# Matmuls of an S5 mixer regrouped by their shape on TensorE

## The chip, the core and the metric

The kernel runs on one core of a Trainium2 chip. The metric is the device time of one execution in microseconds (us); the median of three runs before the change is 2721.66 us (2709.77 to 2725.01). The engines are named as in the profile: PE is TensorE's matmul, PEld its weight load, DVE VectorE, ACT ScalarE, POOL GpSimd, SP the queue that issues most DMAs.

## The reference

One layer of a hybrid decoder for 1024 prompt tokens and 8 single-token samples, of width 1024:

```python
h = x + 0.5 * gt1 * swiglu(modulate(rmsnorm(x)))
proj = modulate(rmsnorm(h)) @ w_in              # S5 inputs, RWKV inputs, gates
y_s5 = s5_branch(proj[..., :512])               # 32 groups of 16 channels, 64 complex states each
y_rwkv = rwkv_branch(token_shift(proj[..., 512:2304]))
m = sigmoid(gates_a) * y_s5 + sigmoid(gates_b) * y_rwkv
h = h + gt2 * (m @ w_out)
h = h + 0.5 * gt3 * swiglu(modulate(rmsnorm(h)))
y = rmsnorm(h)
```

The S5 branch, which the change touches, is a diagonal complex recurrence per group g, with state n and channel c:

```python
bu = einsum('blgc,gnc->blgn', ug, bb)           # complex
xs[t] = lam_bar * xs[t - 1] + bu[t]             # scan over the tokens
y = real(einsum('blgn,gcn->blgc', xs, C)) + d * u
out = (gelu(y) @ glu_v) * sigmoid(gelu(y) @ glu_g)
```

## The kernel before, in words

The kernel works through FFN 1, the input projection, the S5 mixer, the RWKV-7 mixer, the merge and FFN 2. All large products go through `dense` (L144): each product is three matmuls of 128x128 weights against 344 columns (L152 to L154). They are called dense matmuls below. The program's instructions are put on each engine's queue by a scheduler: it takes the code's order with priorities and fills an engine with work of lower priority while something of higher priority isn't ready. Each queue then runs in order.

The S5 mixer (`s5_mix`, L706) works on chunks of 8 tokens: 128 chunk rows of the prompt, and a few rows more for the samples. It runs four quarters of 8 groups each (`s5_quarter`, L616). The tiles of a quarter are single-buffered, and its PSUM tiles come from one tag of four slots. A quarter goes through these steps:

- X transposes and Xs transposes (L628 to L633, recorded at L160): for each of the 8 groups one 128x128 transpose of the prompt (X) and one of 16 rows (Xs), alternating, into three PSUM tiles, each evacuated by ACT (L634).
- State inputs (L640): 16 matmuls with 64 weight columns, evacuated by ACT (L642).
- On DVE the rotation, the scan and the rotation back (L647 to L664), which give the states H. The real half of H is ready after L661, the imaginary one after L664.
- Output products. For each parity g2 of the group (two loops of 4 groups), in PSUM tiles `py` for the prompt and `pz` for the samples: one product of the chunk's own inputs (L687, all 128 rows of the array), two of H (L689, real and imaginary part, 64 rows; the parity says which half of the partitions), then the same three for the samples with 8 weight columns (L691, L693). So the shape on the array changes with nearly every instruction.
- DVE adds the product to `X` (L697) and to the sample rows (L702); ACT applies gelu.

After the quarters, `s5_mix` transposes the result Z (recorded at L160, too) and writes it out. A product in fp32 appears as two records of PE each (x2), a transpose as one. While the S5 mixer runs, PE's queue is filled up with dense matmuls of the RWKV projections (`rwkv_tiles`, called at L1500), which stand behind S5 in the code; their evacuations on ACT and DVE, the tiles `gate`, are raised above S5's work (`offset=30000`), and so stand between the S5 instructions on DVE. When S5 is over, its pool is closed and the RWKV mixer starts (L1510).

Of the kernel before, what the change touches and what calls it, by code (L numbers as in the profile page):

```python
# [19 lines left out]
PSUM = bass.MemoryType.PSUM  # L20
# [5 lines left out]
NP = 1024            # prompt tokens  # L26
NB = 8               # sample sequences
T = NP + NB          # columns
CH = T // 3          # column chunk (one PSUM bank)
LP = NP - 2 * CH     # prompt columns in the last chunk  # L30
# [11 lines left out]
def host_consts():  # L42
    """Identity, ones and masks; they depend on shapes alone."""
    r = np.arange(P)[:, None]
    c = np.arange(P)[None, :]
    c64 = np.arange(64)[None, :]
    m = r % 64
    up = lambda k: (((c64 >> k) - (m >> k)) == 1) & ((c64 >> (k + 1)) == (m >> (k + 1)))
    d = {
        "ident": r == c,  # L50
        "ones": np.ones((P, P)),
        "bones": r // 64 == c // 64,
        "su": r % 64 < c64,
        "ui": r % 64 <= c64,
        "up": np.concatenate([up(4), up(5)], axis=1),
        "i64": m == c64,
    }
    cf = np.concatenate([d[n].astype(np.float32) for n, _ in CF], axis=1)
    return np.ascontiguousarray(cf)
# [6 lines left out]
class Net:  # L66
# [51 lines left out]
    def split(self, hi, lo, src):  # L118
        """hi + lo = src exactly, both with 12 significant bits."""
        nc = self.nc  # L120
        nc.scalar.copy(hi, src)  # L121
        nc.vector.tensor_sub(lo, src, hi.bitcast(F32))  # L122

    def wload(self, *srcs, pool=None):
        """One weight unit of at most 1024 columns as (hi, lo); srcs stack along the middle."""
# [14 lines left out]
    def wcols(self, w, j, n=P):  # L140
        """Column block j of w[(k p), f] as [p, k, n]."""
        return self.wload(w[:, j * n:(j + 1) * n].rearrange("(k p) f -> p k f", p=P))

    def dense(self, terms, c, cols=None):  # L144
        """terms: list of (wh, wl, xh, xl) with [K,128] and [K,cols]; returns PSUM."""
# [11 lines left out]
    def tr(self, out, in_):  # L157
        """out[M, K] = in_[K, M] transposed through the tensor engine."""
# [31 lines left out]
    def ada_steps(self, strips, pool):  # L190
        """Modulation columns of up to four 512-wide strips, side by side in the array; one step per k."""
# [24 lines left out]
    def norm_params(self, q, ks):  # L216
        """a = g (1 + scale) of norm q for the feature tiles ks."""
# [16 lines left out]
    def rsqrt(self, pt, scale, eps_col, pool, floor=None, n=CH, m=P, tmp=None):  # L234
        """1/sqrt(scale * pt + eps) (or of max(pt, floor)), refined by one Newton step."""
# [30 lines left out]
    def norm_apply(self, h, q, c, rs, xh, xl, pool):  # L266
        """One chunk of xh + xl = modulate(rmsnorm(h)) for norm q."""
# [23 lines left out]
    def norm_steps(self, h, q, pool, params=True):  # L291
        """scale(c, tag) and apply(c, xh, xl) of norm q, to be called chunk by chunk."""
# [9 lines left out]
    def resid(self, h, hin, pt, g, d, c):  # L302
        """h[d] = hin[d] + pt * g over one chunk."""
# [12 lines left out]
    def ffn(self, h, q, w1, w3, w2, xh, xl, gp, groups, hooks=None, wp2=None, wide=None):  # L316
        """h += gate * (silu(x w1) * (x w3)) w2 for the hidden tiles of some groups.

        wide: the order of a group's steps: "Hc.e" the hidden products of a chunk, "Oc" its output.
        """  # L320
# [39 lines left out]
    def load_x(self, h, g, pool):  # L360
        """Token tiles 3 g .. 3 g + 2 (the last group ends with the samples), transposed into h."""
# [24 lines left out]
    def final_out(self, h, c, pool, gf):  # L386
        """rmsnorm(h) * g_final for one chunk of tokens, turned token-major first."""
# [28 lines left out]
    def exp_small(self, out, x, pool, n):  # L416
        """exp(x) by range reduction and a polynomial (fp32 accuracy)."""
# [42 lines left out]
    def cmul(self, ore, oim, are, aim, bre, bim, t1, eng=None):  # L460
        """(ore, oim) = a * b; outputs must not alias inputs."""
# [9 lines left out]
    def s5_prep(self, sp):  # L471
        """Discretised parameters; the wide ones go to DRAM scratch by quarters of 8 groups."""
# [9 lines left out]
        # [(g2 n), gp] views of lam_re, lam_im and log_dt  # L482
# [30 lines left out]
        # k = (lam_bar - 1) / lam  # L513
# [15 lines left out]
        # powers lam_bar^tau, tau = 0..8, and the same reversed (7 - s)  # L529
# [12 lines left out]
        # bb[(g2 n), gp, c]  # L542
# [7 lines left out]
        # C as [(g2 n), gp, c]  # L550
# [14 lines left out]
        for g in range(16):  # L565
            nc.sync.dma_start(self.sK[:, 2 * g:2 * g + 2, 0:112], zer)
            # lam^(7-s) bb -> transposed
# [12 lines left out]
            # C lam^tau, sign folded into the imaginary part  # L580
# [6 lines left out]
            # K_tau[c, c']  # L587
# [10 lines left out]
            # e^{i 8 ang q}, q = 0..127  # L598
# [13 lines left out]
    def s5_quarter(self, qd, X, Xs, us, Z, h0, zs, dbc, pool, tag):  # L612
# [15 lines left out]
        for g0, gn in ((0, 3), (3, 3), (6, 2)):  # L628
            pt = self.t(self.pp, [P, gn, 144], tag)
            for q in range(gn):  # L630
                g = 8 * qd + g0 + q
                self.tr(pt[:, q, 0:128], X[:, g].rearrange("p s c -> p (s c)"))
# [33 lines left out]
        # sample states: lam_bar h0 + bb u  # L666
# [8 lines left out]
        # outputs; one PSUM bank per parity of the group, as the parities use different row tiles  # L675
# [4 lines left out]
        xsq = Xs[0:NB, :, 0, :].rearrange("p (gp g2) c -> p g2 gp c", g2=2)  # L680
        for g2 in range(2):
            py = self.t(self.pp, [P, 4, P], tag)
            pz = self.t(self.pp, [NB, 4, 16], tag)
            rows = slice(64 * g2, 64 * g2 + 64)
            for gp in range(4):
                g = 2 * gp + g2
                nc.tensor.matmul(py[:, gp, :], uT[:, g, 0:P], mi[:, g, :], start=True, stop=False)  # L687
                for z in range(2):
                    nc.tensor.matmul(py[:, gp, :], H[rows, gp, z, 0:P],  # L689
                                     co[rows, gp, z, 1:9, :].rearrange("p t c -> p (t c)"), start=False, stop=z == 1)  # L690
                nc.tensor.matmul(pz[:, gp, :], uT[:, g, 128:136], mi[:, g, 0:16], start=True, stop=False)  # L691
                for z in range(2):
                    nc.tensor.matmul(pz[:, gp, :], h0q[rows, z, gp, :], co[rows, gp, z, 1, :],  # L693
                                     start=False, stop=z == 1)
            xv = Xq[:, g2]
            nc.gpsimd.tensor_mul(xv, xv, dq[:, g2].unsqueeze(2).to_broadcast([P, 4, 8, 16]))
            v.tensor_add(xv, xv, py.rearrange("p g (t c) -> p g t c", t=8))  # L697
            for gp in range(4):
                cc = c0 + 32 * gp + 16 * g2
                nc.scalar.activation(Z[:, :, cc:cc + 16], X[:, 8 * qd + 2 * gp + g2], AF.Gelu_apprx_tanh)  # L700
            v.tensor_mul(zq[:, g2], xsq[:, g2], dq[0:NB, g2])
            v.tensor_add(zq[:, g2], zq[:, g2], pz)  # L702
# [3 lines left out]
    def s5_mix(self, X, usT, zout, pool, tag="mm"):  # L706
        """X [128 q, 32 g, 8 s, 16 c] chunk-major inputs, usT [128, 4, 8]; zout(ct, tile) gets z transposed."""
# [12 lines left out]
        # sample rows, once as the first and once as the last token of a chunk  # L720
# [29 lines left out]
        # states out  # L750
# [11 lines left out]
    def rw_init(self, rows, keep, tag):  # L762
        """Per-feature vectors and low-rank weights."""
# [19 lines left out]
    def rw_clear(self, pool):  # L783
        """Zeros around the diagonal blocks of the inverses' scratches."""
# [8 lines left out]
    def rw_lora(self, wad, gd):  # L793
        """wad rows: 64 of wd, 64 of ad; gd: 128 rows (mixed, [128, T])."""
# [6 lines left out]
    def inv_half(x, h):  # L801
        """[64, 4, 64] view of head h; the heads of a scratch lie 4160 apart."""
# [3 lines left out]
    def inv_diag(x):  # L806
        """[32, 16, 16] view of the diagonal blocks of a scratch."""
        return x.rearrange("(q r) -> q r", r=1040)[:, 0:1024].rearrange("q (t s) -> q t s", s=64)[:, :, 0:16]

    def rw_decay(self, sw, tmp, r, exps):  # L810
        """exps(fm, fp, r): r (1 - t)^2 and r (1 + t)^2 are exp(-y), exp(y) for y = e^-0.5 sw and t = tanh(y/2)."""
# [3 lines left out]
        # 1 / (1 - t^2) = (1 + t^2)(1 + t^4)(1 + t^8)(1 + t^16), t < 0.295  # L815
# [13 lines left out]
    def rw_part(n):  # L829
        """Tokens of step n, and its two head pairs with their columns in the step's tiles."""  # L830
# [3 lines left out]
    def rw_prep(self, n, pool):  # L834
        """Decay products, normalised keys and the like for two chunks each of two head pairs."""
# [43 lines left out]
    def rw_solve(self, n, q, pool):  # L879
        """Products of the rows a, r with the rows b, k of four chunks, and the inverses of I - A's 16-blocks.  # L880

        The state is carried without the decay of its last chunk, which a and r take up.  Head h's feature rows
        sit on its own half of the partitions with b's token rows; k's and v's token rows sit on the other.
        """
# [38 lines left out]
        # the 16 x 16 diagonal blocks, one per partition  # L923
# [28 lines left out]
    def rw_quad(self, n, q, sv, pool):  # L952
        """b, k and v with their tokens in the rows, the bonus, and the whole inverse."""
# [6 lines left out]
        # v of each head in the columns of the other half, next to columns that nothing reads  # L960
# [18 lines left out]
        # bonus  # L979
# [8 lines left out]
        # (I - A)^-1 = X P1 P2 from the inverse X of the diagonal blocks, with P1 = I + A1 X and P2 = I + A2 X P1 for  # L988
        # the blocks A1 next to them and A2 below; Y is the transpose
# [604 lines left out]
```

## Time and profile before

| | |
|---|---|
| runs | 2709.77, 2721.66, 2725.01 us |
| span of the profiled execution | 2725.0 us |
| PE busy | 2635.2 us, 97% |
| DVE busy | 1521.9 us, 56% |
| ACT, POOL busy | 804.8 us, 464.3 us |
| mean granted clock of PE over the span | 0.970 of full |
| S5 quarters on PE, first transposes to last product | 1016.90 to 1166.09 us |

The span is as long as the slowest of the three runs (2725.01 us), so nothing of note lies around it. In a timeline each line gives the start and the length of an instruction or of a merged group, engine, line, operation, tiles, weight shape (rows*columns), moving shape and the number of records. Lengths of matmuls overlap, since they are pipelined; what one costs in a full queue is the distance from its start to the start of the next line.

### The profile page before, as it was taken

The page shows a single profiled execution, that of the slowest core. Times are in us where ns is not written, and L with a number is a line of the kernel's source. Part 1 is how long each engine was busy: PE and PEld are TensorE (multiplying, and loading weights), DVE is VectorE, ACT ScalarE, POOL GpSimd, SP SyncE. Part 2 cuts the span into 40 slices and gives each one's busy share as a digit, 9 for nine tenths or more (in the row PEclk, how much of TensorE's full clock was granted, in tenths as well). Part 3 has the DMA queues.
Part 4 walks back from the last instruction along what each step waited for, and adds up shares of the span by engine and source line. Part 5 has one row for each costly group of instructions (what it writes and reads, how often), then busy time and mean ns, then how long its engine had stood idle before and what let it go on. Part 6 is the DMA issues. An engine that isn't in the chain of part 4 may idle for free. (4 is left out here: it accounts for less than half of the span.)

```text
span 2725.0 us, 46727 instructions
## 1 busy us (share of the span) xinstructions
PE 2635.2 (97%) x18175; PEld 2454.6 (90%) x18175; DVE 1521.9 (56%) x4140; ACT 804.8 (30%) x1574; POOL 464.3 (17%) x1123
## 2 busy tenths in 40 slices
PE   7999999999999899999999999899899999999998
PEld 4799999999999898888888889899899999999998
DVE  4533446555555715559989973667854444444435
ACT  4311111111113412256666743221521111111113
POOL 2200003776002300022322210410410000000001
PEclk9999999999999997889999999899899999999999
DMA  7443341222122212333333327543211111111101
GB/s 258 114 139 111 123 128 55 63 66 69 60 68 94 79 54 84 88 105 81 82 79 79 86 64 212 171 120 105 66 55 47 47 47 47 47 47 47 48 24 63
DMA packets 301041, 233.20 MB, mean 86 GB/s; under 512 B 77778, under 2 KB 264947, under 8 KB 300820
## 3 DMA queue, kind: packets, MB, share of 16 engines
q1 hardware_dynamic: 298002, 224.04, 27.9%
q0 software_dynamic: 1920, 5.27, 0.5%
q8 instruction: 143, 2.34, 0.4%
q10 hardware_dynamic: 898, 0.91, 0.1%
q14 instruction: 78, 0.64, 0.1%
HBM read 186.23 MB, written 43.92 MB: 84 GB/s over the span
## 5 line engine op out<-in xcount | busy, mean ns | idle before, releaser
L152 PE MATMUL mm<-xa,wh 128*128 128x344 f32 x2064 | 677.9, 330 | 8.2 <-ACT xa L282 5.6
L154 PE MATMUL mm<-xa,wl 128*128 128x344 f32 x2064 | 674.2, 327 | 3.0 <-DVE wl L122 3.0
L153 PE MATMUL mm<-xb,wh 128*128 128x344 f32 x1848 | 604.0, 327 | 6.2 <-DVE xb L279 2.4
L153 PE MATMUL mm<-xa,wh 128*128 128x344 f32 x1368 | 442.6, 324 | 3.9 <-DVE xa L279 3.1
L121 ACT CAST wh<-wr 128x1024 fp32r<-128x1024 f32 (+1 forms) x190 | 194.6, 1030 | 792.4 <-PE mm L153 695.7
L152 PEld LDWEIGHTS mm<-xa,wh 128*128 128x128 f32 x2064 | 393.7, 191 | 38.5 <-issue 17.3
L307 DVE SCALAR_TENSOR_TENSOR h<-mm,modG,h 128x344 f32<-128x344 f32 (+1 forms) x624 | 351.6, 571 | 126.0 <-PE mm L154 108.7
L154 PEld LDWEIGHTS mm<-xa,wl 128*128 128x128 f32 x2064 | 393.8, 191 | 9.9 <-DVE wl L122 3.5
L152 PE MATMUL mm<-xb,wh 128*128 128x344 f32 x1152 | 371.7, 324 | 5.2 <-ACT xb L121 2.8
L154 PE MATMUL mm<-xb,wl 128*128 128x344 f32 x1152 | 371.1, 323 | 0.0
L153 PEld LDWEIGHTS mm<-xb,wh 128*128 128x128 f32 x1848 | 352.2, 191 | 16.1 <-DVE xb L279 4.7
L122 DVE TENSOR_TENSOR wl<-wr,wh 128x1024 fp32r<-128x1024 f32 (+1 forms) x190 | 230.7, 1214 | 223.3 <-ACT wh L121 218.6
L152 PE MATMUL mm<-gh,wh 128*128 128x344 f32 x1056 | 340.1, 322 | 2.1 <-DVE h L307 1.7
L153 PE MATMUL mm<-gl,wh 128*128 128x344 f32 x1056 | 337.9, 320 | 0.0
L154 PE MATMUL mm<-gh,wl 128*128 128x344 f32 x1056 | 337.9, 320 | 0.0
L328 DVE TENSOR_TENSOR silu<-silu,mm 128x344 f32<-128x344 f32 x132 | 67.5, 511 | 473.8 <-PE mm L154 424.6
L153 PEld LDWEIGHTS mm<-xa,wh 128*128 128x128 f32 x1368 | 260.9, 191 | 5.8 <-DVE xa L279 4.0
L152 PEld LDWEIGHTS mm<-xb,wh 128*128 128x128 f32 x1152 | 219.2, 191 | 7.2 <-ACT xb L282 3.2
L154 PEld LDWEIGHTS mm<-xb,wl 128*128 128x128 f32 x1152 | 219.2, 190 | 0.0
L152 PEld LDWEIGHTS mm<-gh,wh 128*128 128x128 f32 x1056 | 198.7, 188 | 7.5 <-ACT wh L121 2.5
L154 PEld LDWEIGHTS mm<-gh,wl 128*128 128x128 f32 x1056 | 198.7, 188 | 0.2
L153 PEld LDWEIGHTS mm<-gl,wh 128*128 128x128 f32 x1056 | 198.7, 188 | 0.1
(506 smaller groups left out, 3344.9 us busy)
## 6 DMA issues: line engine op xcount, KB each, us to landing
wr<-ffn_w SPq DMA_DIRECT2D x132, 512.0 KB
wada<-w_ada SPq DMA_DIRECT2D x144, 256.0 KB
wr<-w_in SPq DMA_DIRECT2D x34, 512.0 KB
sGate<-gate SPq DMA_DIRECT2D x48, 172.0 KB
gate<-sGate SPq DMA_DIRECT2D x48, 172.0 KB
sMix<-gate SPq DMA_DIRECT2D x36, 172.0 KB
sH<-h SPq DMA_DIRECT2D x8, 516.0 KB
h<-sH SPq DMA_DIRECT2D x8, 516.0 KB
```

What stands on the lines that cost most here:

```text
L121: nc.scalar.copy(hi, src)
L122: nc.vector.tensor_sub(lo, src, hi.bitcast(F32))
L152: nc.tensor.matmul(pt, wh, xh[:, cols], start=q == 0, stop=False)
L153: nc.tensor.matmul(pt, wh, xl[:, cols], start=False, stop=False)
L154: nc.tensor.matmul(pt, wl, xh[:, cols], start=False, stop=q == last)
L307: nc.vector.scalar_tensor_tensor(h[d][:, c0:c0 + np_], pt[:, :np_], g[:, d, 0:1], hin[d][:, c0:c0 + np_], op0=ALU.mult, op1=ALU.add)
L328: nc.vector.tensor_mul(s, s, p3)
```

## The change

The three PSUM tiles of the transposes are taken at once; first all eight X transposes run, then all eight Xs transposes. In the output products, both parities' `py` are taken at once: first all eight products of the inputs, then the sixteen products of H, with the parity in the innermost loop, so that the two halves of the array's rows alternate. The samples' products follow in the same manner, in two `pz` tiles, after the code for the prompt's sum and gelu. Only the first matmul of a bank has `start` now. The arithmetic is the same, and so are the number of instructions on PE and the number of PSUM tiles per quarter (11). The rest of the diff drops comments, which moves the line numbers: by 1 in the quarter's middle, by 13 behind it. All output products of the changed kernel have one line, L685, as a helper issues them.

```diff
-        for g0, gn in ((0, 3), (3, 3), (6, 2)):
-            pt = self.t(self.pp, [P, gn, 144], tag)
+        parts = [(g0, gn, self.t(self.pp, [P, gn, 144], tag)) for g0, gn in ((0, 3), (3, 3), (6, 2))]
+        for g0, gn, pt in parts:
             for q in range(gn):
-                g = 8 * qd + g0 + q
-                self.tr(pt[:, q, 0:128], X[:, g].rearrange("p s c -> p (s c)"))
+                self.tr(pt[:, q, 0:128], X[:, 8 * qd + g0 + q].rearrange("p s c -> p (s c)"))
+        for g0, gn, pt in parts:
+            for q in range(gn):
                 self.tr(pt[:, q, 128:144], Xs[:, g0 + q].rearrange("p s c -> p (s c)"))
             nc.scalar.copy(uT[:, g0:g0 + gn, :], pt)
...
+        py = [self.t(self.pp, [P, 4, P], tag) for _ in range(2)]
+        rows = (slice(0, 64), slice(64, 128))
+        mm = lambda *a, **kw: nc.tensor.matmul(*a, skip_group_check=True, **kw)
         for g2 in range(2):
-            py = self.t(self.pp, [P, 4, P], tag)
-            pz = self.t(self.pp, [NB, 4, 16], tag)
-            rows = slice(64 * g2, 64 * g2 + 64)
             for gp in range(4):
                 g = 2 * gp + g2
-                nc.tensor.matmul(py[:, gp, :], uT[:, g, 0:P], mi[:, g, :], start=True, stop=False)
-                for z in range(2):
-                    nc.tensor.matmul(py[:, gp, :], H[rows, gp, z, 0:P],
-                                     co[rows, gp, z, 1:9, :].rearrange("p t c -> p (t c)"), start=False, stop=z == 1)
-                nc.tensor.matmul(pz[:, gp, :], uT[:, g, 128:136], mi[:, g, 0:16], start=True, stop=False)
-                for z in range(2):
-                    nc.tensor.matmul(pz[:, gp, :], h0q[rows, z, gp, :], co[rows, gp, z, 1, :],
-                                     start=False, stop=z == 1)
+                mm(py[g2][:, gp, :], uT[:, g, 0:P], mi[:, g, :], start=gp == 0, stop=False)
+        for gp in range(4):
+            for z in range(2):
+                for g2 in range(2):
+                    r = rows[g2]
+                    mm(py[g2][:, gp, :], H[r, gp, z, 0:P], co[r, gp, z, 1:9, :].rearrange("p t c -> p (t c)"),
+                       start=False, stop=z == 1)
+        for g2 in range(2):
             xv = Xq[:, g2]
...
-            v.tensor_add(xv, xv, py.rearrange("p g (t c) -> p g t c", t=8))
+            v.tensor_add(xv, xv, py[g2].rearrange("p g (t c) -> p g t c", t=8))
...
+        pz = [self.t(self.pp, [NB, 4, 16], tag) for _ in range(2)]
+        for g2 in range(2):
+            for gp in range(4):
+                g = 2 * gp + g2
+                mm(pz[g2][:, gp, :], uT[:, g, 128:136], mi[:, g, 0:16], start=gp == 0, stop=False)
+        for gp in range(4):
+            for z in range(2):
+                for g2 in range(2):
+                    r = rows[g2]
+                    mm(pz[g2][:, gp, :], h0q[r, z, gp, :], co[r, gp, z, 1, :], start=False, stop=z == 1)
+        for g2 in range(2):
             v.tensor_mul(zq[:, g2], xsq[:, g2], dq[0:NB, g2])
-            v.tensor_add(zq[:, g2], zq[:, g2], pz)
+            v.tensor_add(zq[:, g2], zq[:, g2], pz[g2])
```

PE's queue at the start of the third quarter's output products, before. The PSUM tile s_1587 is the first parity's `py`, s_1588 its `pz`; an x2 is the real and the imaginary part.

```order
L687 MATMUL s_1587_10627<-q_mi_10530,q_uT_10542 128x128
L689 MATMUL s_1587_10627<-q_co_10528,q_H_10608 128x128 x2
L691 MATMUL s_1588_10628<-q_mi_10530,q_uT_10542 8x16
L693 MATMUL s_1588_10628<-q_co_10528,q_h_1586_10625 8x16 x2
L687 MATMUL s_1587_10627<-q_mi_10530,q_uT_10542 128x128
```

The same place now. Here s_1587 and s_1588 are the two parities' `py`, s_1589 and s_1590 their `pz`.

```order
L685 MATMUL s_1587_10627<-q_mi_10530,q_uT_10542 128x128 x4
L685 MATMUL s_1588_10628<-q_mi_10530,q_uT_10542 128x128 x4
L685 MATMUL s_1587_10627<-q_co_10528,q_H_10608 128x128
L685 MATMUL s_1588_10628<-q_co_10528,q_H_10608 128x128
L685 MATMUL s_1589_10665<-q_mi_10530,q_uT_10542 8x16 x4
L685 MATMUL s_1590_10666<-q_mi_10530,q_uT_10542 8x16 x4
L685 MATMUL s_1589_10665<-q_co_10528,q_h_1586_10625 8x16
L685 MATMUL s_1590_10666<-q_co_10528,q_h_1586_10625 8x16
```

The scheduler has put the first pair of products of H (one of each parity) ahead of the samples' products, in this quarter and in the others; the other seven pairs come behind all or some of the samples' products. Between a quarter's state inputs (L640, now L641) and its first output product the queue holds 60, 54, 63 and 62 dense matmuls now, where it held 59, 90, 88 and 88.

PE's queue from the last output products of the first quarter to the transposes of the second, before.

```order
L689 MATMUL s_1547_10323<-q_co_10190,q_H_10270 128x128 x2
L687 MATMUL s_1547_10323<-q_mi_10192,q_uT_10204 128x128
L689 MATMUL s_1547_10323<-q_co_10190,q_H_10270 128x128 x2
L160 MATMUL s_1555_10384<-cf_58,s_X_9655 128x128
L160 MATMUL s_1555_10384<-cf_58,s_Xs_10169 128x16
L160 MATMUL s_1555_10384<-cf_58,s_X_9655 128x128
L160 MATMUL s_1555_10384<-cf_58,s_Xs_10169 128x16
```

The same place now. The tiles s_1554 to s_1556 take the transposes; they lie in the PSUM slots of the quarter before: `py` of the first parity, `py` of the second, and the first `pz`.

```order
L685 MATMUL s_1545_10289<-q_co_10190,q_H_10270 128x128
L685 MATMUL s_1546_10290<-q_co_10190,q_H_10270 128x128
L160 MATMUL s_1554_10376<-cf_58,s_X_9655 128x128 x3
L160 MATMUL s_1555_10377<-cf_58,s_X_9655 128x128 x3
L160 MATMUL s_1556_10378<-cf_58,s_X_9655 128x128 x2
L160 MATMUL s_1554_10376<-cf_58,s_Xs_10169 128x16 x3
L160 MATMUL s_1555_10377<-cf_58,s_Xs_10169 128x16 x3
L160 MATMUL s_1556_10378<-cf_58,s_Xs_10169 128x16 x2
```

The eight X transposes stand together now, straight behind the last pair of products of H. From the first X transpose of the first quarter to the first transpose of Z the queue held 345 dense matmuls before and holds 288 now; the other 57 come behind.

DVE's queue behind the third quarter's output products, before.

```order
L697 TENSOR_TENSOR s_X_9655<-s_X_9655,s_1587_10627 128x4x128
L702 TENSOR_TENSOR s_zs_10187<-s_zs_10187,s_1588_10628 8x4x16
L697 TENSOR_TENSOR s_X_9655<-s_X_9655,s_1589_10661 128x4x128
L702 TENSOR_TENSOR s_zs_10187<-s_zs_10187,s_1590_10662 8x4x16
L658 MEMSET q_H_10777 128x8
```

The same place now.

```order
L699 TENSOR_TENSOR s_X_9655<-s_X_9655,s_1587_10627 128x4x128
L699 TENSOR_TENSOR s_X_9655<-s_X_9655,s_1588_10628 128x4x128
L715 TENSOR_TENSOR s_zs_10187<-s_zs_10187,s_1589_10665 8x4x16
L715 TENSOR_TENSOR s_zs_10187<-s_zs_10187,s_1590_10666 8x4x16
L659 MEMSET q_H_10777 128x8
```

The two large additions follow one another now, and both wait for products that end together.

## Rows read from the trace of the kernel before

**Rows 1.** The page: its first line, and busy time by engine.

```profile
span 2725.0 us, 46727 instructions
PE 2635.2 (97%) x18175; PEld 2454.6 (90%) x18175; DVE 1521.9 (56%) x4140; ACT 804.8 (30%) x1574; POOL 464.3 (17%) x1123
```

**Rows 2.** Stretches: length; busy time and records by engine; PEclk; DMA share; GB/s.

```profile
1016.90:1166.09 149.19, 149.19 (x924) 123.81 (x922) 78.69 (x216) 31.22 (x79) 9.97 (x8) 0.76 0.29 83
1037.35:1061.25 23.90, 23.90 (x99) 18.01 (x98) 6.57 (x18) 4.92 (x16) 2.49 (x2) 0.50 0.29 81
1156.80:1170.45 13.65, 13.65 (x74) 10.62 (x73) 1.78 (x5) 3.84 (x11) 0.00 (x0) 0.50 0.12 37
1166.09:1650.00 483.91, 464.53 (x4778) 395.86 (x4776) 407.00 (x1566) 296.13 (x628) 116.12 (x179) 0.97 0.33 83
```

**Rows 3.** PE by line and form, 1016.90 to 1166.09: dense matmuls.

```profile
L152 PE MATMUL mm<-xa,wh 128*128 128x344 f32 x115 | 38.0, 331 | 0.0
```

**Rows 4.** Timeline of PE: dense matmuls, 26 from the first to the last.

```profile
1024.50 0.32 PE L154 MATMUL mm<-xa,wl 128*128 128x344 f32 x1
...
1028.58 0.32 PE L153 MATMUL mm<-xb,wh 128*128 128x344 f32 x1
```

**Rows 5.** Timeline of PE: output products in the second quarter, clock at full.

```profile
1075.92 0.49 PE L687 MATMUL s<-q_mi,q_uT 128*128 128x128 f32 x2
1076.34 0.71 PE L689 MATMUL s<-q_co,q_H 64*128 64x128 f32 x4
1076.98 0.21 PE L691 MATMUL s<-q_mi,q_uT 128*8 128x16 f32 x2
1077.12 0.25 PE L693 MATMUL s<-q_co,q_h 64*8 64x16 f32 x4
1077.30 0.49 PE L687 MATMUL s<-q_mi,q_uT 128*128 128x128 f32 x2
```

**Rows 6.** Timeline of PE: the same at half the clock.

```profile
1080.94 0.80 PE L687 MATMUL s<-q_mi,q_uT 128*128 128x128 f32 x2
1081.66 1.22 PE L689 MATMUL s<-q_co,q_H 64*128 64x128 f32 x4
1082.82 0.22 PE L691 MATMUL s<-q_mi,q_uT 128*8 128x16 f32 x2
```

**Rows 7.** Timeline of PE: products of H of either parity, first quarter.

```profile
1035.11 0.49 PE L689 MATMUL s<-q_co,q_H 64*128 64x128 f32 x4
1035.53 0.20 PE L693 MATMUL s<-q_co,q_h 64*8 64x16 f32 x2
```

**Rows 8.** Timeline of PE: transposes and state inputs.

```profile
1019.14 0.33 PE L160 MATMUL s<-cf,s_X 128*128 128x128 f32 x1
1019.40 0.29 PE L160 MATMUL s<-cf,s_Xs 16*128 16x16 f32 x2
1019.63 0.33 PE L160 MATMUL s<-cf,s_X 128*128 128x128 f32 x1
...
1021.30 2.23 PE L640 MATMUL s<-q_uT,q_bp 128*64 128x144 f32 x32
1023.46 0.42 PE L154 MATMUL mm<-xa,wl 128*128 128x344 f32 x1
...
1059.74 0.66 PE L152 MATMUL mm<-xa,wh 128*128 128x344 f32 x1
...
1166.09 1.97 PE L160 MATMUL s<-cf,s_Z 128*128 128x128 f32 x8
1167.99 0.27 PE L160 MATMUL s<-cf,s_zs 8*128 8x8 f32 x1
```

**Rows 9.** Timeline of DVE: H complete, first and second quarter; the product added.

```profile
1036.46 0.67 DVE L664 TENSOR_TENSOR q_H<-q_H,q_t 128x512 f32<-128x512 f32 x1
...
1052.73 0.69 DVE L697 TENSOR_TENSOR s_X<-s_X,s 128x512 f32<-128x512 f32 x1 [4.58 <-PE s L689]
...
1074.33 0.68 DVE L664 TENSOR_TENSOR q_H<-q_H,q_t 128x512 f32<-128x512 f32 x1
```

## The prediction

> **What bounds the kernel now.** I read the page's busy times first: PE is busy for 97% of the 2725.0 us and DVE for 56% [rows 1]. A microsecond taken from PE's queue is worth up to a microsecond, unless PE then waits. The change touches only the S5 quarters, so I cut out their stretch in the view of windows, 149.19 us from the first X transpose to the first transpose of Z [rows 2]. PE has no idle time in it, and its mean granted clock is 0.76. The clock has two levels here, so (1 - 0.76) x 2 = 48%, about 72 us, ran at the lower one, 1.2 GHz, instead of 2.4; the first and the last of four such stretches are shown, and each quarter has one. What PE did before each fall: output products, whose shape changes at nearly every instruction.
>
> Dense matmuls take (1028.58 - 1024.50) / 26 = 0.157 us each [rows 4]. The three dense lines have 115 each in the stretch, one of them is shown [rows 3]; 345 x 0.157 = 54 us. The other 149 - 54 = 95 us are S5's own matmuls and what the slow clock adds. This is what the change can cut.
>
> **The change part by part.** One change of shape costs something, and one more matmul of the same shape something else. At the full clock one product of 128 columns (L687, two records) holds the queue for 0.42 us, two of one parity (L689) for 0.64 [rows 5]. So an added product costs 0.22 and the change of shape 0.20. At half the clock they take 0.72 and 1.16 [rows 6]: 0.44 and 0.28. The small ones take 0.14 (two records) and 0.18 (four) [rows 5]: 0.02 a record and 0.10 for the change.
>
> Then, for a quarter at the full clock, with the order printed above:
>
> - Products of the inputs: eight in a group, 0.20 + 8 x 0.22 = 2.0 us.
> - Products of H: eight pairs of opposite parity. The trace before has one such pair: 1035.11 to 1035.53, 0.42 us, as much as one product alone [rows 7]. So the halves of the array work at the same time, and a pair adds 0.22; 0.20 + 8 x 0.22, and 0.20 more as the first pair stands apart: 2.2 us. Bounds: nothing less than 0.22 a pair; 0.44 if pairs overlap only where they stand alone, 1.8 us more a quarter. I take 0.22, the row of the pair itself.
> - Samples: 0.10 + 16 x 0.02 and 0.10 + 32 x 0.02, 1.2 us.
> - Transposes: eight of Z in a row take 1167.99 - 1166.09 = 1.90 us at half the clock [rows 8], so 0.95 at the full one and 0.2 for the change. Two of Xs take at most 0.23 [rows 8], eight 0.9. Together 2.0 us.
> - State inputs, unchanged: 1023.46 - 1021.30 = 2.2 us [rows 8].
>
> That is 9.6 us a quarter, 38 us for four. Today's order without the clock's loss would be 8 x 1.38 (0.42 + 0.64 + 0.14 + 0.18) for the products, 8 x (0.26 + 0.12) for the transposes [rows 5, 8] and 2.2, or 16.3 a quarter, 65 in all. Of the 95 us, grouping takes 27; the other 30 are the clock.
>
> The clock is the large uncertainty. It fell while a good part of PE's time went into changes of shape, and rose during grouped work: 18 transposes in a row brought it from half to full at 1170.45, the end of the last slow stretch (the first nine stand in the rows) [rows 2, 8]. After the change only the samples' 1.2 us and the waits below leave the array nearly empty. I take it that the clock holds, except for two short falls at 2 us each, 4 us.
>
> On the transposes the Trainium skill says otherwise ("TensorE: Matmul & The Clock Gate", Part 4: PE-mode transpose): transposes don't count as busy for the clock. By it the groups of transposes would leave the clock low, some 1 us more a quarter. The rise at 1170.45 after transposes speaks against it here.
>
> What is added are waits of PE, since the queue now reaches things sooner. First, H. Its imaginary half was complete 1036.46 + 0.67 - 1023.46 = 13.7 us after the state inputs in the first quarter, and 1074.33 + 0.68 - 1059.74 = 15.3 us in the second [rows 8, 9]. DVE's work for this is the same, and it takes the dense tiles' evacuations in between. In that time PE now has 60, 54, 63 and 62 dense matmuls (8.5 to 9.9 us), the inputs' products, one pair (0.42) and some of the samples: 12 to 13.5 us, in the first quarter seven dense ones more. It will wait some 0.3, 1, 2 and 2 us: 5.5 us. Behind the waiting pair stands everything else on PE, so these count in full. Second, the X transposes. They need the PSUM of both `py`, which end together; one DVE addition takes 0.69 us [rows 9], so the first three wait 0.8 us and the next three 0.6 more, about half of it beside the transposes already released: 1.1 us at three seams, 3.3. Before, the first parity's addition lay beside the second parity's products. Both together 9 us; bounds 0 (DVE ahead throughout) and 18 (each twice as long).
>
> PE also enters a dense stretch some 20 times, at 0.1 us more: 2 us.
>
> Sum: 95 - 38 = 57, less 2, 9 and 4: 42 us gained. The 57 dense matmuls that no longer fit in the S5 stretch are 9 us of the same work done later; they are neither gain nor loss in this sum. Behind S5, PE is idle for 484 - 465 = 19 us [rows 2]; if they fall in there, up to 9 us are gained on top.
>
> Loading weights could spoil the pairs. By the Trainium skill (the same page, "LDWEIGHTS (loading the stationary operand)") a load of 128 columns takes about 107 ns whatever its rows. If the four loads of a pair ran one after another, a pair would take 0.43 us, and the gain would be 42 - 7 = 35 us. The pair of 0.42 us with the change of shape in it holds four such loads [rows 7], so the row is against it.
>
> The profiled span is that of the slowest run, 3 us above the median. I take the gain off the median: 2721.66 - 42 = 2680 us.
>
> **The rivals.**
>
> Pairs overlap, but the clock falls as today. For it: mixed work with the samples' products stays in every quarter. Against it: far less of the time is spent on changes of shape. At half the clock a quarter is 0.28 + 8 x 0.44 for the inputs, as much and 0.28 for the pairs, 1.2, then 1.90 + 1.1 for the transposes and 4.3 for the state inputs: 16 us, 65 in all. With 4 us for dense matmuls at the slow clock, as today, 2 for entering and 5 for waits (PE is slower, so DVE is less late), 149 - (54 + 65 + 11) = 19 us gained: 2703.
>
> Neither: pairs run one after the other, and the clock falls. Sixteen products of H cost 0.28 + 16 x 0.44 + 0.28 = 7.6 us a quarter instead of 4.1, four times 3.5 us, and the waits grow to 9: 19 - 14 - 4 = 1 us gained, 2721. Only the single pair is against it.
>
> Slower: each alternation of the halves costs a change of shape, 16 times a quarter. Then each product of H costs what a lone one does, 0.72 us at half the clock, 11.5 us a quarter instead of 4.1, and the samples' 16 products 1 us more. That is 8 us more a quarter than in the first rival, 33 in all, 4 for the waits: 19 - 37 = 18 us lost, 2740. It becomes a loss when an alternation costs over half of a change of shape. The single pair speaks against it most of all, since it has one alternation in its 0.42 us.
>
> **How the numbers follow.** The forecast has a chance of 0.75, the rival with the slow clock 0.13, the one with neither 0.07, the slower one 0.05. The forecast's own range goes from 2662 (no waits beyond half of mine, the 57 dense ones in idle time) to 2696 (waits of 18 us, pairs at 0.44). The range reaches on to the first rival: 2662 to 2706. Below 2708 the kernel is faster by over 0.5%, which is about what a measurement can tell from no change: 0.75 + 0.11 = 0.86. Within 0.5%: 0.02 + 0.06 = 0.08. Slower: 0.06, the last rival and a little of the one before it.
>
> **What would show it.** In the profile after, the stretch from the first X transpose to the first transpose of Z is about 100 us long, with a mean clock over 0.9; eight pairs of H take about 2 us and not 3.7; PE waits for DVE's H before the second pair, and at the X transposes for the addition. A clock of 0.75 in that stretch makes the first rival right. Pairs of 0.4 us each at the full clock mean that they don't overlap. If the stretch is as short as I say and the time is not, the gain was given back behind S5, and I would have been wrong that PE sets that stage.

## The result, and the profile after

The changed kernel takes 2673.76 us, the median of 4 runs (2672.56 to 2675.56), against 2721.40 of the kernel before beside it. The ratio is 0.9839 with a 95% interval of 0.9817 to 0.9861. Its profiled span is 2673.8 us, 51.2 less than that of before. The first two lines of the page, beside [rows 1]:

```profile
span 2673.8 us, 46729 instructions
PE 2571.4 (96%) x18175; PEld 2409.4 (90%) x18175; DVE 1517.5 (57%) x4140; ACT 806.8 (30%) x1576; POOL 454.5 (17%) x1123
```

PE does the same 18175 matmuls and is busy 64 us less. The view of windows shows where (columns as in [rows 2]): first the S5 stretch, then as long a stretch behind it as in [rows 2].

```profile
1014.35:1103.20 88.85, 83.87 (x867) 77.58 (x865) 75.94 (x205) 27.70 (x73) 10.14 (x8) 1.00 0.45 124
1103.17:1587.08 483.91, 458.23 (x4746) 388.38 (x4747) 404.62 (x1576) 299.29 (x632) 108.56 (x179) 0.97 0.33 84
```

The S5 stretch fell from 149.19 to 88.85 us, its mean clock rose from 0.76 to 1.00, and PE now has 5 us of idle time in it. The lines view of that stretch, beside [rows 3]:

```profile
L152 PE MATMUL mm<-xa,wh 128*128 128x344 f32 x96 | 31.0, 323 | 0.0
```

There are three such lines, so 288 dense matmuls where 345 stood: 57 moved out, 57 x 0.157 = 9 us. S5's own part is 88.8 - 288 x 0.157 = 43.6 us instead of 95. With the rest of the span:

| us | before | after | difference |
|---|---|---|---|
| up to the first X transpose | 1016.9 | 1014.4 | -2.5 |
| S5, its own part | 95.0 | 43.6 | -51.4 |
| S5, dense matmuls in between | 54.2 | 45.2 | -9.0 |
| behind S5 | 1558.9 | 1570.6 | +11.7 |

Nine of the 11.7 us behind S5 are the dense matmuls that moved there. The timeline of PE in the first quarter (start, length, instruction, records; in brackets the idle time before it and what ended it), beside [rows 5, 7, 8]:

```profile
1014.35 1.05 PE L160 MATMUL s<-cf,s_X 128*128 128x128 f32 x8
1016.99 0.64 PE L160 MATMUL s<-cf,s_Xs 16*128 16x16 f32 x8 [1.12 <-DVE s_Xs L627]
1018.37 2.23 PE L641 MATMUL s<-q_uT,q_bp 128*64 128x144 f32 x32
...
1030.05 1.95 PE L685 MATMUL s<-q_mi,q_uT 128*128 128x128 f32 x16
1031.92 0.49 PE L685 MATMUL s<-q_co,q_H 64*128 64x128 f32 x4
1032.35 0.56 PE L685 MATMUL s<-q_mi,q_uT 128*8 128x16 f32 x16
1032.83 0.56 PE L685 MATMUL s<-q_co,q_h 64*8 64x16 f32 x32
...
1035.28 1.83 PE L685 MATMUL s<-q_co,q_H 64*128 64x128 f32 x28 [0.60 <-DVE q_H L665]
1037.05 0.88 PE L160 MATMUL s<-cf,s_X 128*128 128x128 f32 x6
1038.31 0.44 PE L160 MATMUL s<-cf,s_X 128*128 128x128 f32 x2 [0.39 <-DVE s_X L699]
1038.68 0.66 PE L160 MATMUL s<-cf,s_Xs 16*128 16x16 f32 x8
```

Read it by the distance from one start to the next. Seven pairs with H (28 records) take 1037.05 - 1035.28 = 1.77 us, with one change of shape in it. Without that change, at the prediction's 0.20, it is 0.22 a pair, where the two products of a pair cost 0.44 one after the other [rows 5]. The waits of PE in the S5 stretch (us in total, times, longest):

```profile
PE s L685 <- DVE q_H L665: 2.5, 4, 0.7
PE s L160 <- DVE s_X L699: 1.2, 3, 0.5
PE s L160 <- DVE s_Xs L627: 1.1, 1, 1.1
```

### The profile page after: what moved, and what is told of

It is laid out like the page before. It is cut to its first block, busy times and chain, and to the rows that moved or that the text cites. A ratio compares the mean times of both kernels' runs of the same rounds, so it can differ in the third digit from the quotient of the medians.

```text
span 2673.8 us, 46729 instructions
## 1 busy us (share of the span) xinstructions
PE 2571.4 (96%) x18175; PEld 2409.4 (90%) x18175; DVE 1517.5 (57%) x4140; ACT 806.8 (30%) x1576; POOL 454.5 (17%) x1123
```

## The experiments

Two things were open: what holds the clock at full, and whether the stage behind S5 is really neutral. Each of e1 to e4 undoes one part of the change.

**e1: transposes grouped, products as before.**

```diff
 (transposes as changed)
+for g2 in range(2):
+    for gp in range(4):   # input, 2 x H, sample input, 2 x sample state
```

> The transposes grouped as in the change, the output products in the order of before. Theory (half of the gain is time saved at changes of shape, half is the clock, which falls during the mixed output products): the products stay at 11 us a quarter at the full clock and near 18 at half, the clock still falls in each quarter, and the transposes save about 2 us a quarter: 8 to 10 us, 2712 us, mean clock in the S5 stretch about 0.78. Rival (the clock is decided in the transposes and state inputs): mean clock above 0.88 and 2700 us or less.

Measured: 2702.25 us, ratio 0.9933 (0.9907 to 0.9958). In the view of windows: its S5 stretch, most of its first two stretches at half the clock, and the output products of its first quarter, with the dense matmuls and transposes between them:

```profile
1015.45:1150.44 134.99, 133.83 (x922) 115.52 (x921) 79.68 (x216) 30.48 (x79) 10.06 (x8) 0.83 0.32 92
1067.00:1084.00 17.00, 17.00 (x96) 13.62 (x96) 3.69 (x10) 3.65 (x13) 2.51 (x2) 0.51 0.23 60
1101.00:1121.00 20.00, 20.00 (x100) 15.56 (x101) 3.98 (x15) 4.19 (x13) 2.50 (x2) 0.51 0.34 90
1031.18:1043.78 12.60, 12.60 (x111) 9.65 (x110) 7.21 (x21) 2.63 (x7) 0.00 (x0) 1.00 0.46 138
```

Some 45 us still ran at half the clock, against 72 before. This lies between what the theory (2712 us, 0.78) and its rival (2700 or less, above 0.88) expected: grouped transposes alone don't hold the clock, but one of the four falls is gone, that of the first quarter. There the build put most of the samples' products ahead of the large ones, and the quarter passes at 1.00 with its 32 changes of shape; in the other three, where small products stand between the large ones, the clock falls.

**e2: products as changed, transposes as before.** Each X transpose is followed by its Xs transpose again.

```diff
-for q in range(gn): self.tr(pt[:, q, 0:128], X[...])     # all X, then all Xs
+for q in range(gn): self.tr(pt[:, q, 0:128], X[...]); self.tr(pt[:, q, 128:144], Xs[...])
```

> The output products grouped as in the change, the transposes alternating as before. Theory: the clock holds during the products; alternating transposes at the full clock cost 3.3 us a quarter where the changed kernel's grouped ones took 1.6, so about 7 us slower than the changed kernel: 2681 us. If the alternating transposes make the clock fall by themselves, 8 us more, 2689 us. Together with e1 the two parts should add up to the 48 us within 10 us; where the clock couples them, they add up to less or more.

Measured: 2678.48 us, ratio 0.9839 (0.9817 to 0.9861), near the 2681 of the theory, but not quite by its terms. S5 takes 98.62 us at a mean clock of 0.97, its own part 49.6, 6.0 more than in the change; one fall of the clock, 6.8 us from the last quarter's transposes on, is in it. Behind S5, e2 then gained 7 us on the change for equal work (table below). So the products alone bring back most of the clock. The gains of e1 and e2, 18 and 42 us, add up to 59, 12 more than the change's 48 and outside the expected 10: each of the two parts also saves some of the same slow clock, and the stage behind S5 differs.

**e3: as changed, but the two parities one after the other,** in the products with H and in the samples'.

```diff
-for gp in range(4): for z in range(2): for g2 in range(2):
+for g2 in range(2): for gp in range(4): for z in range(2):
```

> The changed kernel, but with the products of H (and the samples' ones) of one parity all before those of the other: still grouped by shape, no alternation of the halves. Theory (alternating pairs run at the same time, 0.22 us a pair): 16 products of H then take 16 x 0.22 + 0.20 = 3.7 us instead of 2.2 a quarter, so 6 to 7 us slower than the changed kernel at an unchanged clock of 1.00: 2680 us. Rival (pairs don't overlap, or alternating costs nothing): the same time as the changed kernel, 2674. Rival (the overlap is what keeps the clock up): mean clock of the S5 stretch below 0.9 and 2695 us or more.

Measured: 2660.72 us, ratio 0.9772 (0.9750 to 0.9793). It is 13 us faster than the change, where the theory had it 7 slower. The timeline of its first quarter:

```profile
1034.76 0.87 PE L685 MATMUL s<-q_co,q_h 64*8 64x16 f32 x32
1037.20 3.05 PE L685 MATMUL s<-q_co,q_H 64*128 64x128 f32 x28 [0.29 <-DVE q_H L665]
1040.18 1.09 PE L160 MATMUL s<-cf,s_X 128*128 128x128 f32 x8
```

The 28 records take 2.98 us instead of 1.77, so the pairs of the change do overlap, and here S5's own part is 46.1 us, 2.5 more. (The longer products alone would make it some 6 more, but PE's idle time in the stretch is 2.3 us shorter.) But the part behind S5 takes 1549.5 us against 1570.6. That is the second open question, taken up from e5 on.

**e4: pairs side by side, but not grouped:** per pair of groups two input products, two pairs with H, then the samples'.

```diff
+for gp in range(4):
+    (2 inputs) ; (2 pairs with H) ; (2 sample inputs) ; (2 pairs of samples)
```

> Transposes as in the change; output products with the two parities side by side but taken group pair by group pair, so the shape changes four times for each of four pairs (16 times a quarter; before 32 times, the changed kernel some 5 times). Theory of price: 0.64 + 0.64 + 0.18 + 0.26 = 1.7 us for each group pair, 6.9 a quarter, where the changed kernel took 5.1: 7 us slower than it if the clock holds, 2681 us. If changes of shape as such bring the clock down, 11 us a quarter at half the clock and the state inputs at half as well: about 2700 us.

Measured: 2680.20 us, ratio 0.9846 (0.9820 to 0.9872). Its timeline:

```profile
1039.62 0.71 PE L686 MATMUL s<-q_mi,q_uT 128*128 128x128 f32 x4
1040.26 0.72 PE L686 MATMUL s<-q_co,q_H 64*128 64x128 f32 x8
1040.90 0.71 PE L686 MATMUL s<-q_mi,q_uT 128*128 128x128 f32 x4
```

Two input products take 0.64 us and two pairs 0.64, as the price list of the prediction has it (0.20 + 2 x 0.22). S5 takes 103.81 us at a clock of 1.00, its own part 49.8. So 16 changes of shape a quarter, with the halves of the array side by side, don't bring the clock down; the 32 of before are not tested by this.

**e5, e6: only one of the two groups in series,** the samples' (e5) or the products with H (e6), each as in e3. **e7:** the loop over H's real and imaginary halves outermost. Their edits:

```diff
 e5: pz only   +for g2 in range(2): for gp in range(4): for z in range(2):
 e6: py only   +for g2 in range(2): for gp in range(4): for z in range(2):
 e7: py only   +for z in range(2): for gp in range(4): for g2 in range(2):
```

> The changed kernel, only the samples' 16 state products of a quarter issue one parity after the other. Behind S5 VectorE issues its instructions almost in the changed kernel's order (1 in 1000 of the first 1500 stand elsewhere; against e3's order every second one). Theory (the order that the build gives the RWKV stage decides the 13 us between the change and e3): S5 90 us (88.8 + 4 x 0.3), the stage behind it 1570 as in the changed kernel, 2675 us in all. Rival (series of small products is what made e3 faster): about 2660.

> The changed kernel, only the 16 products with H of a quarter issue one parity after the other; the samples' stay in pairs. Behind S5 TensorE's and VectorE's instructions stand in the order of e3, row for row. Theory: S5 92 us (93.35 - 4 x 0.3), the stage behind it 1549.5 as in e3, 2659.5 us in all, 14 faster than the change although the group of H costs 1.2 us more a quarter. Rival (order behind S5 does not matter, S5 alone sets the time): 2673.8 + 4 x 1.2 = 2679.

> The changed kernel with the loop over real and imaginary halves outside: the four pairs with H's real half first, then the four with its imaginary half, which VectorE finishes later. Behind S5 both engines issue in the order of e2 (it differs in 5 of 1000 TensorE rows). Theory: the waits for H in the stretch (2.5 us) fall to under 1, S5 87 us; the stage behind S5 costs e2's 1554.6 + 0.157 for each dense product that S5 no longer holds, about 7 less than in the changed kernel; 2665 us in all (2662 to 2668). Rival (order does not matter): 2672.

Measured: e5 2676.87 us, 0.9846 (0.9828 to 0.9864); e6 2661.93 us, 0.9793 (0.9772 to 0.9815); e7 2672.89 us, 0.9832 (0.9811 to 0.9853). The first two are as the theory had them (in e5, S5 took 88.1 us and not 90). e7 missed its range of 2662 to 2668, and its time is the 2672 of the rival. The stages tell that this is chance: behind S5 it is 9.3 us faster than the change for equal work, as the theory had it (table below), but S5 takes 96.4 us and not 87. It holds 316 dense matmuls instead of 288, and these are PE's waits in it:

```profile
PE s L641 <- ACT q_uT L635: 2.7, 1, 2.7
PE s L685 <- DVE q_H L665: 2.7, 2, 1.4
PE s L160 <- DVE s_Xs L627: 1.1, 1, 1.1
```

The waits for H didn't shrink (2.7 us against 2.5): PE reaches the imaginary half sooner by as much. And a new wait of 2.7 us came before one short fall of the clock, 3.4 us at half; S5's own part is 46.8 us.

**e8: series and changes of shape as before for the products with H, the samples' products taken out** and issued behind them.

```diff
 for g2 in range(2):
     for gp in range(4):
         (1 input) ; (2 x H)
-        (1 sample input) ; (2 x sample state)
```

> Transposes grouped as changed; the products with H as before (one parity after the other, each 128x128 product followed by its two products of half the rows, so 32 changes of shape a quarter), but the samples' products taken out of that and issued behind them. Theory (small products between the large ones leave the array too idle, and that is what brings the clock down): the clock holds at 1.00 or falls once, S5 about 105 to 110 us. Rival (the series of half-row products with changes of shape does it): it falls at least three times as in e1, half clock over 30 us, S5 about 120 to 130. The time of the whole kernel is not the test, since the order behind S5 is a new one (2680 to 2700).

Measured: 2703.49 us, ratio 0.9940 (0.9917 to 0.9963). Its S5 stretch, and products in it:

```profile
1016.09:1125.25 109.16, 107.22 (x917) 95.81 (x915) 81.87 (x215) 30.50 (x80) 11.07 (x8) 1.00 0.40 113
```

```profile
1037.41 0.71 PE L685 MATMUL s<-q_co,q_H 64*128 64x128 f32 x4
1038.05 0.49 PE L685 MATMUL s<-q_mi,q_uT 128*128 128x128 f32 x2
1038.46 0.71 PE L685 MATMUL s<-q_co,q_H 64*128 64x128 f32 x4
```

The rows are those of [rows 5] without the small products, at the same 0.42 and 0.64 us, and the clock is 1.00 throughout: of the two, the theory is the one that holds. Such a run of large products in series lasts 8.5 us in the second quarter and doesn't lower the clock. (The changes of shape among the large products are 16 a quarter, not the 32 of the expectation.) Against e1 this takes the small products from between the large ones and, with them, their half of the changes of shape; no run takes these two apart. With them go all falls of the clock, and the stretch is 26 us shorter. The whole kernel is no faster than e1 for it, and 3 us above the expected 2680 to 2700: behind S5 it takes 1575.1 us against e1's 1550.1.

**e9, e10, e11: the products with H in series in some quarters, in pairs in the others.**

```diff
+if qd in (0, 3):     # e9;  e10: qd in (1, 3);  e11: qd in (0, 1, 3)
+    (as e6)
+else:
+    (as changed)
```

> The changed kernel, the products with H one parity after the other in the quarters 0 and 3, in pairs in 1 and 2. The build gives the stage behind S5 the changed kernel's order (of the first 1500 VectorE instructions 3 in 1000 stand elsewhere). Theory (that order sets what the stage behind S5 takes): S5 88.8 + 2 x 1.2 = 91 us, the stage behind it with equal dense work as in the change and e5 (1557 to 1562), 2677 us in all. Rival (the order is no cause, only S5 and chance are): the same time as e10 within 2 us.

> As e9, with the quarters 1 and 3 in series instead: the same instructions and the same price within S5. The build gives the stage behind S5 the order of e2 and e7 (2 in 1000 stand elsewhere). Theory: the stage behind S5 with equal dense work as in e2 and e7 (1552.4 to 1554.6), 4 to 8 us less than in e9; 2670 us in all. Rival: as e9.

> As e9, with the quarters 0, 1 and 3 in series. The build gives the stage behind S5 the order of e3 and e6 (3 in 1000 stand elsewhere). Theory: the stage behind S5 with equal dense work as in those two (1542.6 and 1543.1), 15 to 19 us less than in e9; S5 itself 1.2 us more than in e9; 2660.5 us in all. Rival (order no cause): 1.2 us slower than e9, about 2678.

Measured: e9 2680.45 us, 0.9852 (0.9821 to 0.9883); e10 2670.55 us, 0.9828 (0.9798 to 0.9858); e11 2660.34 us, 0.9786 (0.9760 to 0.9812). (e9's four runs range from 2669.97 to 2680.95, three of them at 2680 or 2681.) These three are the test of the order: S5 takes 91.8, 92.4 and 92.2 us, and the kernels lie 10 and 20 us apart. (The 10 between e9 and e10 rest on those three runs; the fourth lies among e10's, 2669.82 to 2672.88. e11's runs end at 2661.86, clear of both.) The table puts all kernels together by the order that the build gave the stage behind S5: within a row at most 5 in 1000 of the first 1500 VectorE instructions stand elsewhere, between rows 300 or more. "Equal work" is the length of that stage less 0.157 us for each dense matmul below 345 in S5.

| same order behind S5 | behind S5, equal work |
|---|---|
| before, e4 | 1558.9, 1559.2 |
| after, e5, e9 | 1561.7, 1557.2, 1561.6 |
| e2, e7, e10 | 1554.6, 1552.4, 1553.2 |
| e3, e6, e11 | 1542.6, 1543.1, 1542.3 |
| e1 alone; e8 alone | 1549.9; 1574.0 |

With one profiled execution each, the stage repeats to 4.5 us within an order, and between orders it spreads over 32. The kernels of a row also leave nearly the same number of dense matmuls to that stage (S5 holds 344 or 345 of them in the first row, then 285 to 288, 311 to 316, and 301). The number alone doesn't explain the times: 301 lies between the others and is the fastest, and e1 with 344 takes 9 us less than before and e4. Where the time goes is looked for in the first 200 us behind S5. First the changed kernel, the window and then the largest waits of PE from 50 to 150 us behind S5:

```profile
1103.17:1303.17 200.00, 179.59 (x1599) 155.51 (x1599) 165.95 (x640) 124.97 (x259) 50.18 (x81) 0.92 0.35 90
```

```profile
PE sv L859 <- DVE qx L952: 6.0, 1, 6.0
PE ch L1036 <- DVE SUV L1050: 3.4, 2, 2.8
PE mm L154 <- DVE inv L872: 2.6, 1, 2.6
```

And e11, whose line numbers are one lower:

```profile
1108.05:1308.05 200.00, 189.61 (x1710) 166.15 (x1704) 169.89 (x654) 127.50 (x262) 49.53 (x84) 0.97 0.39 102
```

```profile
PE sv L858 <- DVE qx L951: 1.7, 1, 1.7
PE qd L1009 <- DVE qx L951: 1.1, 2, 0.9
PE mm L154 <- DVE wl L122: 1.0, 1, 1.0
```

In the changed kernel PE is idle for 20.4 of the 200 us, in e11 for 10.4. It also runs (1 - 0.92) x 2 = 16% of them at half the clock, 32 us, against 6%, 12 us; a microsecond at half the clock loses half of one, so that is another 10 us. The two together are about the 19.4 us between the kernels in the table. From 50 to 150 us behind S5, DVE is busy for 91.0 us and PE for 84.4 in the changed kernel (93.2 and 93.8 in e11), so DVE is the busier side there; over the whole 200 us PE is. The waits behind the inverse `qx` are 6.8 us in this window against 3.3. At the other end e8 has a clock of 0.88 and 25 us of idle time in its 200 us. That the stage goes with the order is shown by the kernels that share it, and e9 to e11 were forecast by it; how much of the difference is the waits, and how much the clock that fell behind them, no run takes apart.

## Why the prediction was right, point by point

The time was forecast as 2680 us and is 2673.76, with the likeliest case as its cause: the pairs overlap and the clock holds. The gain over the median was 42 us by forecast and 48 by measurement; it was larger than forecast in S5 and partly given back behind it. By the terms of its sum:

- **S5's products and transposes, 38 us.** Measured per quarter, from start to start: inputs 1.9, H 0.43 + 1.77, samples 1.0, transposes 1.7, state inputs 2.2, together 9.0 where 9.6 stood. That is 36 us in all. Part of it is the samples' 16 products with 64 rows (32 records): their halves overlap too, 0.56 us in length against 0.87 in series (e3). The other part is the transposes, 1.7 where 2.0 stood.
- **Pairs at 0.22 us.** It is 0.25 measured with the change of shape shared out and 0.22 without it, against 0.43 in series in e3. The weight loads of these records (PEld), first the change's, then e3's:

```profile
1035.28 1.64 PEld L685 LDWEIGHTS s<-q_co,q_H 64*128 64x128 f32 x28 [0.88 <-DVE q_H L665]
1037.20 2.86 PEld L685 LDWEIGHTS s<-q_co,q_H 64*128 64x128 f32 x28 [0.57 <-DVE q_H L665]
```

In series that is 2.86 / 28 = 0.10 us a load, in pairs 0.06, so loads for the two halves overlap. The Trainium skill ("TensorE: Matmul & The Clock Gate", "LDWEIGHTS (loading the stationary operand)") gives about 107 ns for a load of 128 columns, and the row in series agrees. What the rows refute is the prediction's "if", that the four loads of a pair run one after another.
- **Entering dense stretches, 2 us.** What is left of the 43.6 us beside 36 and the 5.0 idle is 2.6.
- **Waits, 9 us.** 4.8 us measured. The term was nearly twice too large: for H it had 0.3 + 1 + 2 + 2 (which is 5.3, not the 5.5 written), and it is 0.5 to 0.7 each time, at the same place; at the X transposes it is 1.2 and not 3.3. One wait wasn't in the sum: the eight Xs transposes of the first quarter now come in a row and meet DVE's copy into Xs, 1.1 us.
- **The clock, 30 of the 57 us to gain, less 4 for two short falls.** No fall came. This was called the large uncertainty, and rightly. The prediction's reason, the share of time in changes of shape, separates the kernels only thinly. By its price list that share is 0.60 of 1.38 us for each group before, 0.40 of 1.06 in e8 and 0.60 of 1.72 for each pair of groups in e4, and the last two stay at 1.00. Taking the small products out from between the large ones (e8), pairing (e4) or grouping in series (e3) each ended the falls of before and e1, and each also lowers the number of changes. So which of the two brings the clock down is open; e1's first quarter, at 1.00 with 32 changes, speaks for the small products between large ones. Not every fall fits that: the first one before (1037.35) came behind a run mostly of small products (1032.81 to 1036.63), and nearly the same run passed in e1 (1031.18 to 1034.91). Single short falls are left in e2, where Xs transposes stand between the large X ones, in e7 behind a wait, and in e9 among the last quarter's products with H in series, which pass in e3, e6, e10 and e11.
- **The transposes and the clock.** Here eight X and eight Xs transposes, in rows of two to eight with a wait among them or just before, passed at 1.00 in each quarter. e1 has them too and falls elsewhere, so no run shows grouped transposes lowering the clock. In e9 it rose from half to full at 1111.98 us, behind 3.6 us of nothing but transposes of the result Z. The Trainium skill ("TensorE: Matmul & The Clock Gate", "Part 4: PE-mode transpose") has it that transposes don't count as busy for the clock; that rise, like the one at 1170.45 in the prediction, is against it.
- **S5 in sum:** 95 - 53 = 42 us of gain forecast, 51.4 measured; the nine us are the waits (4), the clock (4) and the products (2), less the 0.6 for entering.
- **The 57 dense matmuls behind S5, neutral.** 11.7 us came back there, 9 for them and 2.7 more, while the part ahead of S5 was 2.5 shorter. So as a sum the term was right. As a reason it wasn't: the stage behind S5 is no constant. The build orders it anew for each kernel, and e9 to e11 differ by 8 and 19 us there with S5 equal within 0.7. That the changed kernel got an order about as slow as that of before (1561.7 against 1558.9) was luck. With the order of e3 it would have come out some 19 us lower, at about 2655 by these rows, below the stated range from 2662, and nothing in the sum would have said why.

Of the rivals, the one with the slow clock wanted 65 us for S5's own work and a clock of 0.75; neither is there. The one in which pairs run one after the other is refuted by 1.77 us against 2.98 for the same 28 records, and the slower one, a change of shape for each alternation, by the same row.

The best kernels of the study are e11, e3 and e6, at 2660 to 2662 us. They are not better in S5 (own part 44.9 to 46.1 us against 43.6), they got a better order behind it.

## What to carry to other kernels

Where a stretch of TensorE alternates small products with large ones, take the small ones out or put independent row halves side by side, and look at the granted clock before counting instructions: by the prediction's split 30 of the 57 us to gain here were the clock. Either remedy held the clock here; which feature of the mix lowers it stays open. Then compare stage by stage, with the deferred work subtracted, before a difference of 10 us is put down to the edit. When a build schedules all stages together, an edit in one stage reorders the next, and kernels with the same order there are the control for it.

## What the runs showed that was not expected

- The clock holds through 16 changes of shape a quarter (e4, e8: 1.00), and is 0.83 on average where the samples' products of 0.14 and 0.18 us stand between the large ones in series, with 32 changes a quarter (e1).
- The overlap of the two parities reaches the smallest products: 16 products with 64 rows (32 records) in 0.56 us, 0.87 in series.
- The 1550 us behind S5 moved by up to 32 us (1542 to 1574 for equal work) with the instruction order that the build gave them, with PE idle and the clock low in its first 200 us. With S5 nearly equal, e9 to e11 show 19 us of this.
